# Three of eleven channel groups of gate and up as block products with seven multiplications of eight

## The chip, the cores and the metric

The kernel runs on one core of a Trainium2 chip. The core's engines are in-order queues that wait for one another through semaphores: TensorE (PE, matmuls, with weight loads listed apart as PEld), VectorE (DVE), ScalarE (ACT), GpSimd (POOL, used for a few operations and as a DMA queue) and SyncE (SP, a DMA queue). The metric is the device time of one execution in microseconds (us); less is better.

## The reference

One decoder layer over 256 tokens and 16 meta tokens in float32: an RWKV-7 branch and a forgetting-attention branch, a gated merge, the output projection w_o, and a SwiGLU feed-forward. The change lies in the last two:

```python
merged = g_a * (y_a @ w_a) + g_b * (y_b @ w_b)
h = h + merged @ w_o
gate, up = jnp.split(_rms(h, n2) @ w_gu, 2, axis=-1)
return h + (jax.nn.silu(gate) * up) @ w_dn
```

h has 2048 channels, gate and up have 5632 each, and w_gu is 2048 x 11264.

## The kernel before

Every matrix product is done to float32 accuracy in three matmuls: an operand is split into a rounded high part and the remainder (hi and lo), and hi x hi, lo x hi and hi x lo are added up in PSUM. Weights come in tiles of 128 x 1024 elements (512 KB): SP fetches one into raw (four buffers), ACT writes its high part wh, DVE subtracts to get wl (four buffers of each, so the preparation can be up to three tiles ahead of PE). The function run takes a list of jobs, each a load and a multiplication; it writes the load of the next job ahead of the multiplication of the one before. The order on each engine is that of a scheduler, which puts out instructions by its own estimate of when they are ready.

**w_o** (tm_jobs): tokens on the partitions, four groups of 512 channels, eight weight tiles each. The function post adds x into hh (the residual, two tiles of tokens, kept in SBUF to the end), sums its squares, turns it with PE transposes (hT), scales it by n2 (htmp), and splits it into hts, 16 channel tiles with a high and a low part of 256 tokens side by side. The norm's factor rs2 is spread over the partitions as rsb2 (spread, two transposes) and multiplied in after the product.

**Gate and up** (lines 1402 to 1423): eleven groups j of 512 columns, first gate (tile gt), then up (tile up), eight weight tiles each. PE holds a 128 x 128 piece of the weights and streams hts through it (mm2, lines 440 to 443): 512 columns against wh (both parts of hts in one matmul) and 256 against wl, so 16 + 16 matmuls in a tile. Gate accumulates in the four PSUM banks called main, up in the four called aux. At a group's end halves (lines 447, 448) adds the two halves of a bank (ACT copies, DVE adds); DVE multiplies by rsb2, ACT takes silu, and the product of gate and up is split into ach and acl (44 channel tiles, transposed: channels on the partitions).

**Down**: 22 blocks i of 256 channels. Twelve of them (SLOW) are plain. Ten (FAST) use a block product with seven multiplications for eight, which needs four sums of token quarters (sums_of_tokens, made at the end of an up group, written to DRAM as ss by POOL and fetched again as sst and into ach and acl) and sums of weight quarters (tt, from a fetch q). Before, FAST is 0 to 9, so the groups j = 0 to 4 make the sums. The results of the seven products are added to hh at the end of each half (sums_of_products).

Of the kernel before, what the change touches and what calls it, by code (L numbers as in the profile page):

```python
# [60 lines left out]
PLACE_T = (8, 16)  # L61

# [5 lines left out]
FAST = list(range(10))  # L68
SLOW = list(range(10, 22))
ORDER = [SLOW[:4] + [i for pair in zip(FAST, SLOW[4:] + FAST[-1:]) for i in pair],  # L70
         SLOW[:1] + [i for pair in zip(FAST, SLOW[1:]) for i in pair] + SLOW[11:]]
QUICK = [FAST[:-1], FAST]

# [42 lines left out]
def hybrid_block(ctx, tc, A, out, dbg=None):  # L116
# [1185 lines left out]
    hh = hp.tile([P, 2, D], F32, tag="hh", name="hh")  # L1302

    ht_pool = tc.tile_pool(name="ht", bufs=1, reuse_waits="tile")
    ht = ht_pool.__enter__()
    ht.tile([P, 32], F32, tag="shift", name="shift")
    hts = ht.tile([P, KT, 2, L], F32R, tag="hts", name="hts")
    ss2 = hp.tile([P, 2, 4], F32, tag="ss2", name="ss2")
    rs2 = hp.tile([P, 2], F32, tag="rs2", name="rs2")
    rsb2 = hp.tile([P, T], F32, tag="rsb2", name="rsb2")  # L1310

# [28 lines left out]
    for j in range(4):  # L1340
# [3 lines left out]
        def post(t, ps, j=j, js=js):  # L1344
            nc.vector.tensor_tensor(hh[:, t, js], ps, hh[:, t, js], op=ALU.add)
            jk = ht.tile([P, 512], F32, tag="jk", name=f"jk{j}{t}", bufs=2)
            nc.scalar.activation(jk, hh[:, t, js], AF.Square, accum_out=ss2[:, t, j:j + 1])
            if t == 0:
                return
            for k in range(4 * j, 4 * j + 4):  # L1350
# [3 lines left out]
                tmp = ht.tile([P, T], F32, tag="htmp", name=f"htmp{k}", bufs=3)  # L1354
                nc.vector.tensor_scalar(tmp, pt, vc("n2", k), None, op0=ALU.mult)
                split(hts[:, k, 0, NMETA:], hts[:, k, 1, NMETA:], tmp)
        run(tm_jobs(A["w_o"][0][:, js], KT, mgh, mgl, post, f"wo{j}"))
# [5 lines left out]
    obs = [ht.tile([P, P], F32, tag="ob", name=f"ob{t}", bufs=2) for t in range(2)]  # L1363
    for t in range(2):
        nc.vector.tensor_copy(obs[t], rs2[:, t:t + 1].to_broadcast([P, P]))

    def spread():

        prb = aux_ps("prb")[:, :T]
        for t in range(2):  # L1370
            pe_tr(prb[:, t * P:(t + 1) * P], obs[t], ident)
        nc.vector.tensor_copy(rsb2, prb)
        return
        yield
    spawn(spread(), SPREAD)
    dump("hh", hh)
# [11 lines left out]
    ssd = {}  # L1388

    def sums_of_tokens(i, u0, u1):  # L1390

        (a11, a21), (a12, a22) = ((u[:, :P], u[:, P:]) for u in (u0, u1))
        sx = ht.tile([P, 512], F32, tag="jk", name=f"sx{i}", bufs=2).rearrange("p (n c) -> p n c", n=4)
# [8 lines left out]
    for j in range(DFF // 512):  # L1402
        gs = [ht.tile([P, T], F32, tag="ga", name=f"ga{j}{m}", bufs=8) for m in range(4)]

        def post_gate(pss, gs=gs):
            for g, ps in zip(gs, pss):
                halves(g, ps)
                nc.vector.tensor_tensor(g, g, rsb2, op=ALU.mult)
                nc.scalar.activation(g, g, AF.Silu)
# [14 lines left out]

# [214 lines left out]
```

## Time and profile before

| | us |
|---|---|
| median of 3 runs | 1515.87 (1515.62 to 1516.62) |
| the profiled execution's own time | 1515.74 |
| its span, first to last instruction | 1514.0 |

| stage, us from the span's start | PE | DVE | ACT | share of DMA |
|---|---|---|---|---|
| 0 to 627, input projection and branches | 623.7 | 507.4 | 364.7 | 0.61 |
| 627 to 717, mostly branch projections | 90.0 | 62.4 | 43.2 | 0.73 |
| 854 to 1031, gate and up with token sums | 177.0 | 121.5 | 93.6 | 0.74 |
| 1031 to 1298, gate and up, start of down | 267.0 | 162.4 | 132.0 | 0.67 |
| 1298 to 1398, first half of down | 98.9 | 90.1 | 56.0 | 0.68 |
| 1398 to 1514, second half of down | 112.3 | 98.5 | 58.7 | 0.54 |

The table gives the busy time of each engine in each stage. "Busy" for PE counts a matmul until its modelled end, so it is the gaps that say something: a stage whose PE is busy for its whole length had no wait in front of a matmul. An answer of the trace has a start, a duration, the engine, the line, the operation with output <- inputs, and in brackets the idle time ahead of it with what ended that. A row of a window holds the bounds, the length, the busy times of PE, weight loads, DVE, ACT and POOL, the granted clock, the share of the DMA engines and GB/s.

### The profile page before, as it was taken

The page shows a single profiled execution, that of the slowest core. Times are in us where ns is not written, and L with a number is a line of the kernel's source. Part 1 is how long each engine was busy: PE and PEld are TensorE (multiplying, and loading weights), DVE is VectorE, ACT ScalarE, POOL GpSimd, SP SyncE. Part 2 cuts the span into 40 slices and gives each one's busy share as a digit, 9 for nine tenths or more (in the row PEclk, how much of TensorE's full clock was granted, in tenths as well). Part 3 has the DMA queues.
Part 4 walks back from the last instruction along what each step waited for, and adds up shares of the span by engine and source line. Part 5 has one row for each costly group of instructions (what it writes and reads, how often), then busy time and mean ns, then how long its engine had stood idle before and what let it go on. Part 6 is the DMA issues. An engine that isn't in the chain of part 4 may idle for free.

```text
span 1514.0 us, 26216 instructions
## 1 busy us (share of the span) xinstructions
PE 1505.9 (99%) x10056; PEld 1335.8 (88%) x10056; DVE 1130.9 (75%) x2014; ACT 817.8 (54%) x1234; POOL 123.5 (8%) x222
## 2 busy tenths in 40 slices
PE   9999999999999999999999999999999999999999
PEld 9999999999989888998888888888888888788887
DVE  7888699689779857875665776666566566789987
ACT  7664565475465545553555555555455455455553
POOL 2112202202202000000000000000000001000000
PEclk9999999999999999999999999999999999999999
DMA  8567456646645856777566777777666666966762
GB/s 272 166 167 212 119 155 183 173 118 178 189 126 149 224 153 204 241 257 216 181 182 183 227 219 226 208 214 214 195 186 189 195 185 207 326 197 202 224 213 86
DMA packets 214111, 293.82 MB, mean 194 GB/s; under 512 B 24737, under 2 KB 134833, under 8 KB 213985
## 3 DMA queue, kind: packets, MB, share of 16 engines
q1 hardware_dynamic: 202048, 277.25, 61.3%
q0 software_dynamic: 7040, 10.49, 2.2%
q10 hardware_dynamic: 4896, 4.40, 0.9%
q8 instruction: 79, 1.29, 0.3%
q14 instruction: 48, 0.39, 0.1%
HBM read 279.60 MB, written 12.49 MB: 193 GB/s over the span
## 4 chain that ended last, share of the span: by engine, by line
PE 97%; DVE 2%; DMA 0%; issue 0%; ACT 0%; SPq 0%; DVEq 0%
PE gt L441 11%; PE up L441 11%; PE zg L441 8%; PE gt L443 5%; PE up L443 5%; PE dn L1459 4%; PE dn L1457 4%; PE dn L1458 4%; PE zg L443 4%; PE f L441 2%; PE br L365 2%; PE br L366 2%; PE br L367 2%; PE f L365 2%; PE wo L1332 2%; PE wo L1334 2%
## 5 line engine op out<-in xcount | busy, mean ns | idle before, releaser
L336 DVE TENSOR_TENSOR wl<-raw,wh 128x1024 fp32r<-128x1024 f32 x450 | 550.2, 1227 | 271.7 <-ACT wh L335 270.6
L335 ACT ACTIVATE wh<-raw 128x1024 fp32r<-128x1024 f32 x450 | 475.7, 1059 | 442.4 <-PE up L441 121.8
L441 PE MATMUL gt<-hts,wh 128*128 128x512 f32 x704 | 243.0, 393 | 0.0
L441 PE MATMUL up<-hts,wh 128*128 128x512 f32 x704 | 242.7, 392 | 0.0
L443 PE MATMUL gt<-hts,wl 128*128 128x256 f32 x660 | 184.7, 280 | 0.0
L443 PE MATMUL up<-hts,wl 128*128 128x256 f32 x660 | 184.5, 280 | 0.0
L441 PE MATMUL zg<-xhl,wh 128*128 128x512 f32 x512 | 181.2, 399 | 0.0
L441 PEld LDWEIGHTS gt<-hts,wh 128*128 128x128 f32 x704 | 129.9, 188 | 25.2
L441 PEld LDWEIGHTS up<-hts,wh 128*128 128x128 f32 x704 | 129.9, 188 | 25.2
L443 PE MATMUL zg<-xhl,wl 128*128 128x256 f32 x480 | 134.3, 280 | 0.0
L443 PEld LDWEIGHTS up<-hts,wl 128*128 128x128 f32 x660 | 125.3, 190 | 1.8
L443 PEld LDWEIGHTS gt<-hts,wl 128*128 128x128 f32 x660 | 125.3, 190 | 1.8
L441 PEld LDWEIGHTS zg<-xhl,wh 128*128 128x128 f32 x512 | 94.3, 188 | 18.7 <-issue 0.7
L1457 PE MATMUL dn<-wh,ach 128*128 128x512 f32 x257 | 101.2, 394 | 0.0
L1459 PE MATMUL dn<-wl,ach 128*128 128x512 f32 x257 | 100.3, 393 | 0.6 <-DVE wl L511 0.4
L1458 PE MATMUL dn<-wh,acl 128*128 128x512 f32 x257 | 100.7, 392 | 0.0
L443 PEld LDWEIGHTS zg<-xhl,wl 128*128 128x128 f32 x480 | 90.9, 189 | 1.2
L365 PE MATMUL f<-xhl,wh 128*128 128x272 f32 x256 | 75.9, 296 | 0.0
L510 ACT ACTIVATE wh<-tt 128x1024 fp32r<-128x1024 f32 x38 | 40.4, 1063 | 64.9 <-PE dn L1458 60.0
L367 PE MATMUL f<-xhl,wl 128*128 128x272 f32 x256 | 73.6, 288 | 0.0
L366 PE MATMUL f<-xhl,wh 128*128 128x272 f32 x256 | 73.6, 288 | 0.0
L511 DVE TENSOR_TENSOR wl<-tt,wh 128x1024 fp32r<-128x1024 f32 x38 | 46.5, 1224 | 21.1 <-ACT wh L510 20.9
(496 smaller groups left out, 3171.0 us busy)
## 6 DMA issues: line engine op xcount, KB each, us to landing
raw<-in_w_gate_up_dram SPq DMA_DIRECT2D x176, 512.0 KB, 4.3
raw<-in_w_in_dram SPq DMA_DIRECT2D x160, 512.0 KB, 3.9
raw<-in_w_down_dram SPq DMA_DIRECT2D x50, 512.0 KB, 4.3
q<-in_w_down_dram SPq DMA_DIRECT2D x38, 512.0 KB, 5.0
raw<-in_w_o_dram SPq DMA_DIRECT2D x32, 512.0 KB, 4.4
raw<-in_w_branch_a_dram SPq DMA_DIRECT2D x16, 512.0 KB, 4.7
raw<-in_w_branch_b_dram SPq DMA_DIRECT2D x16, 512.0 KB, 4.7
ss<-sr POOLq DMA_DIRECT2D x10, 512.0 KB, 5.0
```

The source lines that it names most:

```text
L335: nc.scalar.activation(th, rr, AF.Copy)
L336: nc.vector.tensor_tensor(tl, rr, th.bitcast(F32), op=ALU.subtract)
L365: nc.tensor.matmul(ps, wh, ah, start=first, stop=False)
L366: nc.tensor.matmul(ps, wh, al, start=False, stop=False)
L367: nc.tensor.matmul(ps, wl, ah, start=False, stop=last)
L441: nc.tensor.matmul(ps.rearrange("p (a t) -> p a t", a=2), wh, act, start=first, stop=last)
L443: nc.tensor.matmul(ps[:, :T], wl, act[:, 0, :], start=False, stop=False)
L510: nc.scalar.activation(hi, src, AF.Copy)
L511: nc.vector.tensor_tensor(lo_, src, hi.bitcast(F32), op=ALU.subtract)
L1457: nc.tensor.matmul(o, a[0], hi, start=first, stop=False)
L1458: nc.tensor.matmul(o, a[1], hi, start=False, stop=False)
L1459: nc.tensor.matmul(o, a[0], lo_, start=False, stop=last)
```

## The change

Eight of the eleven groups (PLAIN, j = 0 to 7) stay as they were in their products. Three (BLOCK, j = 8 to 10) are computed with tokens on the partitions: a weight tile of 256 rows is taken as a block of two by two quarters (two of channels in, two of 256 columns), the tokens as two by two quarters (two of channels, two of 128 tokens), and seven products do for eight (groups bg for gate, bh for up). PE holds a 128 x 128 piece of tokens and streams 256 columns of weights; each of the seven products is three matmuls. Four aux banks hold the seven results of a group in halves, so a block group's gate and up follow one another on them. A weight tile is now prepared in two parts: 768 columns as fetched, and four quarters of sums (tt).

The sums of tokens that these products need are made in the w_o stage, at the end of each group (hs0 to hs7), written to DRAM by POOL and fetched to "homes": four tiles of their own and the parts of ach and acl where j = 6 and 7 will be stored. To make room, hh is written to DRAM (hhd, by ACT's queue) and fetched again in down (hh2). Gate and up of the plain groups both use main, and work on all 1024 elements of a group at once where they worked on 256 (except halves). At the end of a block group seven additions collect the products (sums); after up the result is turned by eight transposes (turn), and split into ach and acl. The block jobs are spread over the first 112 of the 128 plain jobs. FAST becomes 6 to 15, so that only plain groups (j = 3 to 7) make the sums for down.

```diff
-FAST = list(range(10))
-SLOW = list(range(10, 22))
+FAST = list(range(6, 16))
+SLOW = [i for i in range(22) if i not in FAST]
...
+PLAIN = list(range(8))
+BLOCK = list(range(8, 11))
+HOMES = 112
+FOLD = 9000
...
+    def sums_of_tokens(pool, tag, bufs, name, u0, u1, turned):
...
+        for n, x_, y_ in ((2, a11, a21), (3, a12, sx[:, 1])):
+            nc.vector.tensor_tensor(sx[:, n], x_, y_, op=ALU.subtract)
+        split(sr[:, 0], sr[:, 1], sx)
+        d = dp.tile([P, 2, 4, P], F32, tag=name, name=name)
+        nc.gpsimd.dma_start(d, sr.bitcast(F32))
+        return d
...
+            nc.scalar.dma_start(hhd[:, t, js], hh[:, t, js])
...
+                if k % 2:
+                    hsd.append(sums_of_tokens(wo, "hs", 2, f"hs{k // 2}", *tmps[-2:], True))
...
+    for h_, d in zip(homes, hsd):
+        nc.gpsimd.dma_start(h_, d)
...
+            nc.vector.tensor_tensor(g, g, rb, op=ALU.mult)
+            nc.scalar.activation(g, g, AF.Silu)
...
+            for i in range(2):
+                if 2 * j + i in FAST:
+                    ssd[2 * j + i] = sums_of_tokens(gu, "hb", 1, f"ss{2 * j + i}", ub[:, 2 * i], ub[:, 2 * i + 1],
+                                                    False)
...
+                def load0():
+                    raw = wp.tile([P, 1024], F32, tag="raw", name="raw", bufs=RAWB)
+                    nc.sync.dma_start(raw.rearrange("p (k c) -> p k c", c=512), kblock(src))
+                    w = parts(768)
+                    split(*w, raw[:, 256:])
+                    t = gu.tile([P, 1024], F32, tag="tt", name="tt", bufs=2)
...
+                def load1():
+                    w = parts(1024)
+                    split(*w, tt[0])
+                    return w
...
+                    nc.tensor.matmul(o, a[0], hi, start=opens, stop=False, skip_group_check=True)
+                    nc.tensor.matmul(o, a[1], hi, start=False, stop=False, skip_group_check=True)
+                    nc.tensor.matmul(o, a[0], lo_, start=False, stop=closes, skip_group_check=True)
...
+                def mul0(w):
...
+                    product("p1", token(i, 0, 0), w, 0)
+                    product("c12", s_of(3), w, 1)
+                    product("c11", token(i, 1, 0), w, 2)
+
+                def mul1(w):
+                    product("p5", s_of(0), w, 0)
+                    product("p7", s_of(2), w, 1)
+                    product("p6", s_of(1), w, 2)
+                    product("c21", token(i, 1, 1), w, 3)
...
+            for o, a, b in ((at(0, 0), ps["c11"], u), (u, ps["p6"], u), (v, ps["p5"], u), (at(0, 1), ps["c12"], v),
+                            (u, ps["p7"], u), (at(1, 0), ps["c21"], u), (at(1, 1), ps["p5"], u)):
+                nc.vector.tensor_tensor(o, a, b, op=ALU.add)
...
+        begin, stop = (HOMES * n // len(groups), HOMES * (n + 1) // len(groups))
+        for i, block in enumerate(g):
+            after = begin + 5 + (stop - begin - 6) * i // (len(g) - 1)
+            todo += plain[at:after]
+            at = after
+            todo += block
...
+        if cg == 0:
+            nc.gpsimd.dma_start(hh, hhd)
```

Three places show what moves. The first is PE in the fifth weight tile of the first gate group, from the two transposes of spread on; before, it reads:

```order
L395 MATMUL prb_10000<-ident_69,ob0_9868 128x128
L395 MATMUL prb_10000<-ident_69,ob1_9869 128x128
L441 MATMUL gt0_3_9899<-hts_9127,wh_9961 128x512
L443 MATMUL gt0_3_9899<-hts_9127,wl_9962 128x256
L441 MATMUL gt0_3_9899<-hts_9127,wh_9961 128x512
L443 MATMUL gt0_3_9899<-hts_9127,wl_9962 128x256
L441 MATMUL gt0_0_9896<-hts_9127,wh_9983 128x512
```

and now (bg82 and bg80 are the first block group's banks, home0 the first home):

```order
L400 MATMUL prb_10110<-ident_69,ob_9964 128x128 x2
L446 MATMUL gt0_3_10005<-hts_9129,wh_10067 128x512
L448 MATMUL gt0_3_10005<-hts_9129,wl_10068 128x256
L446 MATMUL gt0_3_10005<-hts_9129,wh_10067 128x512
L448 MATMUL gt0_3_10005<-hts_9129,wl_10068 128x256
L1500 MATMUL bg82_10124<-wh_10090,hts_9129 128x256
L1501 MATMUL bg82_10124<-wh_10090,hts_9129 128x256
L1502 MATMUL bg82_10124<-wl_10091,hts_9129 128x256
L1500 MATMUL bg80_10122<-wh_10090,home0_9967 128x256
```

The sixth plain tile has moved behind the first block tile, whose fourth matmul needs home0.

The second is the two engines that this block waits for. POOL's queue, from the sums of the last two w_o groups to the last home:

```order
L1430 DMA ach_9959<-hs4_9720 128x1024
L1430 DMA acl_9960<-hs5_9743 128x1024
L1334 DMA hs6_9914<-hs6r_9907 128x1024
L1334 DMA hs7_9937<-hs7r_9930 128x1024
L1430 DMA ach_9959<-hs6_9914 128x1024
L1430 DMA home0_9967<-hs0_9318 128x1024
L1430 DMA home1_9968<-hs1_9341 128x1024
```

and DVE at the same time (hs7r is the last sum of tokens, raw_10088 the first block's weights, tt its sums of quarters):

```order
L516 TENSOR_TENSOR hs7r_9930<-hs7r_9930 128x512
L1392 TENSOR_SCALAR ms2_9940<-rs2_9123 128x2
L516 TENSOR_TENSOR wl_10091<-raw_10088,wh_10090 128x768
...
L1482 TENSOR_TENSOR tt_10094<-raw_10088 128x512
L1482 TENSOR_TENSOR tt_10159<-raw_10153 128x512
L1486 TENSOR_TENSOR tt_10094<-raw_10088,tt_10094 128x256
L1418 COPY rsb2_9124<-prb_10110 128x256
L1487 TENSOR_TENSOR tt_10094<-raw_10088,tt_10094 128x256
L1486 TENSOR_TENSOR tt_10159<-raw_10153,tt_10159 128x256
L1487 TENSOR_TENSOR tt_10159<-raw_10153,tt_10159 128x256
L516 TENSOR_TENSOR wl_10119<-tt_10094,wh_10118 128x1024
```

None of these rows but the norm's stood here before. home0, though its data is written long before, stands behind a fetch of hs6, which waits for the write of hs6; and the first tt row waits for the writes of hs6 and hs7, whose memory it takes.

The third is SP's queue at the start of down, around the first fetch for a fast block (q). Before:

```order
L326 DMA raw_14698<-in_w_down_dram 128x2x512
L326 DMA raw_14710<-in_w_down_dram 128x2x512
L1488 DMA q00_14477<-in_w_down_dram 128x1024 x2
L1488 DMA q01_14643<-in_w_down_dram 128x1024 x2
L326 DMA raw_14779<-in_w_down_dram 128x2x512
```

and now:

```order
L331 DMA raw_15198<-in_w_down_dram 128x2x512
L331 DMA raw_15210<-in_w_down_dram 128x2x512
L331 DMA raw_15279<-in_w_down_dram 128x2x512
L331 DMA raw_15291<-in_w_down_dram 128x2x512
L1637 DMA q06_14976<-in_w_down_dram 128x1024 x2
L1637 DMA q07_15143<-in_w_down_dram 128x1024 x2
```

The q fetches have moved behind two more weight fetches, each of which waits until DVE has given back a raw buffer.

More of the change, by code (lines that the diff above doesn't have):

```diff
@@ L61 @@
 PLACE_T = (8, 16)
+SHIFT = 128
 LANES = 108
@@ L1301, in hybrid_block @@
     hp = hp_pool.__enter__()
[L1302 to L1307, printed above, removed]
     ss2 = hp.tile([P, 2, 4], F32, tag="ss2", name="ss2")
@@ L1362, in hybrid_block @@
     rsqrt_small(hp, rs2, ms2, [P, 2], "rst2")
[L1363 to L1376, printed above, removed]
+    wo_pool.__exit__(None, None, None)
     mg_pool.__exit__(None, None, None)
@@ L1402, in hybrid_block @@
[L1402 to L1409, printed above, removed]
-        def post_up(pss, gs=gs, j=j):
-            us = []
-            for m, (g, ps) in enumerate(zip(gs, pss)):
-                ub = ht.tile([P, T], F32, tag="ub", name=f"ub{j}{m}", bufs=2)
-                halves(ub, ps)
-                nc.vector.tensor_tensor(ub, ub, rsb2, op=ALU.mult)
-                nc.vector.tensor_tensor(ub, ub, g, op=ALU.mult)
-                split(ach[:, 4 * j + m, :], acl[:, 4 * j + m, :], ub)
-                us.append(ub)
-                if m % 2 and 2 * j + m // 2 in FAST:
-                    sums_of_tokens(2 * j + m // 2, *us[m - 1:])
-        run(cm_jobs(wgu[:, j * 512:(j + 1) * 512], KT, hts, NMETA, T, post_gate, name=f"gt{j}"))
-        run(cm_jobs(wgu[:, DFF + j * 512:DFF + (j + 1) * 512], KT, hts, NMETA, T, post_up, alloc=aux_ps, name=f"up{j}"))
+    gu_pool = tc.tile_pool(name="gu", bufs=1, reuse_waits="tile")
@@ new lines, in hybrid_block, with spread, home @@
+    gu = gu_pool.__enter__()
+    obs = gu.tile([P, 2, P], F32, tag="bu", name="ob")
+    for t in range(2):
+        nc.vector.tensor_copy(obs[:, t], rs2[:, t:t + 1].to_broadcast([P, P]))
+    def spread():
+        prb = aux_ps("prb")[:, :T]
+        for t in range(2):
+            pe_tr(prb[:, t * P:(t + 1) * P], obs[:, t], ident)
+        nc.vector.tensor_copy(rsb2, prb)
+        return
+        yield
+    spawn(spread(), SPREAD)
+    def home(t):
+        return t.rearrange("p (a n c) -> p a n c", a=2, n=4)
@@ L1431, in hybrid_block @@
+    plain = [job for j in PLAIN for job in plain_jobs(j)]
+    groups = [g for j in BLOCK for g in block_jobs(j)]
+    todo, at = [], 0
+    for n, g in enumerate(groups):
+        begin, stop = (HOMES * n // len(groups), HOMES * (n + 1) // len(groups))
[4 more added lines that the diff above has]
+            todo += block
+    run(todo + plain[at:])
     wdn = A["w_down"][0]
@@ L1438, in hybrid_block @@
     sst = dn.tile([P, len(fast), 2, 3, P], F32R, tag="sst", name="sst")
+    hh = dn.tile([P, 2, D], F32, tag="hh", name="hh2")
     def sums_of(i):
```

119 lines of the change are left out of this document (107 added, 12 removed).

## The prediction

> **What bounds the kernel now.** I read the page's busy line and chain first, then the windows of the stages, then the rows of the stage that is changed.
>
> ```profile
> span 1514.0 us, 26216 instructions
> PE 1505.9 (99%) x10056; PEld 1335.8 (88%) x10056; DVE 1130.9 (75%) x2014; ACT 817.8 (54%) x1234; POOL 123.5 (8%) x222
> PE 97%; DVE 2%; DMA 0%; issue 0%; ACT 0%; SPq 0%; DVEq 0%
> 831.87:1275.87 444.00, 444.00 (x2561) 391.57 (x2561) 288.62 (x450) 228.75 (x331) 15.25 (x28) 1.00 0.69 204
> 831.87 0.46 PE up L441 x2
> 1275.87 0.46 PE up L441 x2
> ```
>
> TensorE (PE) is 97% of the chain of waits that ended last. In the window over most of gate and up it has no idle time, at the full clock, and VectorE (DVE, third pair of numbers) works 288.6 of 444 us, 65%. The last two rows, of the chain, are the same place in the first and in the last up group, twenty groups of eight weight tiles apart: 444.0 / 160 = **2.775 us of PE for one plain weight tile**. A change here is worth what it takes off PE, less every wait that it puts in front of PE.
>
> **What PE gains.** Of 11 x 16 tiles, 48 become block tiles. Each plain one is 16 matmuls of 512 columns and 16 of 256. Each block tile is 21 matmuls of 256 columns, each with its own weight load. The branch stage already runs such a stream:
>
> ```profile
> 605.87:697.31 91.44, 91.44 (x774) 91.35 (x773) 70.03 (x89) 47.63 (x50) 0.00 (x0) 1.00 0.76 249
> 650.01 0.28 PE L365 MATMUL br<-ybs,wh 128*128 128x256 f32 x1
> 651.43 0.28 PE L365 MATMUL br<-ybs,wh 128*128 128x256 f32 x1
> 788.48 0.39 PE L441 MATMUL gt<-hts,wh 128*128 128x512 f32 x1
> 790.07 0.40 PE L441 MATMUL gt<-hts,wh 128*128 128x512 f32 x1
> ```
>
> Between the two br rows lie 12 matmuls: 1.42 / 12 = 0.1183 us each. A block tile takes 21 x 0.1183 = 2.484 us, and saves 0.291. The window says why it isn't the eighth that counting columns promises (0.347): weight loads are busy 91.35 of 91.44 us. So 48 x 0.291 = **-14.0 us**. Unequal column patterns could move the pitch; bounds are the 0.347 of the count (-16.7) and a gain of half (-7).
>
> The page "TensorE: Matmul & The Clock Gate" of the Trainium skill, section "Back-to-back issue gap", gives N/2.4 + 2.5 ns for a lone matmul, 109 ns at 256 columns; by it a block tile takes 2.29 us and the change saves 23 us. The same section says that in a stream of load and matmul both set the spacing, and the 118 ns of the br rows agree with that, so the row is used.
>
> PE is also given 24 transposes (turn, eight for each of three channel groups). From 788.48 to 790.07 stand two pairs of plain matmuls (2 x 0.347) and eight transposes: (1.59 - 0.69) / 8 = 0.112, so **+2.7 us**. Bare PE time falls by 11.3.
>
> **What DVE gets.** A plain tile costs DVE one subtraction of 1024 elements; a block tile costs 768, 512, 256, 256 and 1024.
>
> ```profile
> 1305.26 2.35 DVE L336 TENSOR_TENSOR wl<-raw,wh 128x1024 fp32r<-128x1024 f32 x2
> 1307.53 0.68 DVE L511 TENSOR_TENSOR wl<-q,wh 128x512 fp32r<-128x512 f32 x1
> 1308.13 0.68 DVE L1512 TENSOR_TENSOR tt<-q,tt 128x512 f32<-128x512 f32 x1
> 811.36 0.74 DVE L448 TENSOR_TENSOR ga<-ga,gt 128x256 f32<-128x256 f32 x2
> 812.03 0.75 DVE L1408 TENSOR_TENSOR ga<-ga,rsb 128x256 f32<-128x256 f32 x2
> L1396 DVE TENSOR_TENSOR sx<-ub,ub 128x128 f32<-128x128 f32 x10 | 2.8, 285 | 0.0
> 1335.00:1355.00 20.00, 20.00 (x88) 16.30 (x87) 17.22 (x19) 10.95 (x12) 0.00 (x0) 1.00 0.63 209
> 1300.00:1310.00 10.00, 9.07 (x39) 6.78 (x38) 9.93 (x11) 6.00 (x7) 0.00 (x0) 1.00 1.04 351
> ```
>
> From start to start back to back: 1024 elements 2.27 / 2 = 1.135, 512 0.60, 256 0.67 / 2 = 0.335, and 0.87 between for 768; 128 as listed, 0.285. A block tile: 0.87 + 0.60 + 0.67 + 1.135 = 3.28. The stage after: 128 plain tiles 145.3; 48 block tiles 157.4; eight plain posts of eight 256 and four 1024 57.6; three block posts of fourteen 256 and four 512 21.3; ten token sums of four 128 and one 512 17.4. That is 399 us beside PE's 128 x 2.775 + 48 x 2.484 + 2.7 = 477, or **84%**. With the listed durations instead of start to start, as for rows that wait for the row ahead, it is some 443, 93%. The down stage is the measure: at 17.22 of 20, 86%, PE loses nothing; at 9.93 of 10 it loses 0.93. So DVE's sum as such is charged nothing, and what stops DVE in its order is.
>
> One such stop is new: the two sums of a plain block now share one buffer (hb), so the second one's first subtraction waits until the first one's write has landed, and all weight tiles queue behind it on DVE. The write and the next instruction that needs it:
>
> ```profile
> 841.16 0.78 POOL L1400 DMA_DIRECT2D ss<-sr  x1 [307.62 <-DVE sr L511]
> 845.94 0.55 POOL L1443 DMA_DIRECT2D ach<-ss  x1 [4.00 <-DMA ss<-sr]
> ```
>
> 4.8 us, against some three weight rows between (3 x 1.135 = 3.4): up to 1.4 us of DVE lost, five times. DVE is up to three tiles (about 8 us) ahead of PE, and spends that on the burst of the up post just there. I charge half, **+3.5 us**, between 0 (the lead covers it) and 19 (the third rival).
>
> **The first block.** In before the last split of hts ends at 794.95, and the first group begins at 788.48. POOL writes hs6 and hs7 from there and fetches the homes behind them.
>
> ```profile
> 790.68 1.26 DVE L1355 TENSOR_SCALAR htmp<-hT,vcol 128x256 f32<-128x256 f32 x3
> 794.53 0.42 DVE L511 TENSOR_TENSOR hts<-htmp,hts 128x256 fp32r<-128x256 f32 x1
> sst<-ss POOLq DMA_DIRECT2D x10, 384.0 KB, 13.3
> ```
>
> PE reaches the block after five tiles, eight transposes and two of spread: 788.5 + 5 x 2.775 + 1.2 = 803.6, and asks for home0 0.35 us later. DVE ahead of the hs6 write: from 790.7 on eight htmp and hts rows of about 0.36, seven subtractions of 0.285 and a split of 0.60, so 796. The write lands at 800.9, the queue then issues ach (which waits for it) and home0 at about 801.5, and home0 lands 4.8 later, at 806.3: PE waits 2.4. With the 13.3 us that ten loads together took, it is 814.8 and 10.9. Five loads of 512 KB go out in a row here, nearer to one than to ten: **+4 us**. At the same time DVE stands at tt, whose memory waits for the hs6 and hs7 writes (until 803), and then has 4.4 us of rows to the block's second tile: 807.4, hidden behind home0.
>
> **The rest.** Gate and up now both accumulate in main, so ten plain groups follow one another on the same banks.
>
> ```profile
> 810.09 0.37 ACT L447 ACTIVATE ga<-gt 128x256 f32<-128x256 f32 x1
> 811.99 0.23 PE up L441
> ```
>
> In before the first bank was read out by 811.36 + 0.41 = 811.77, and the next group began at 811.99: covered by 0.2, with the four additions now together. If DVE is one weight row late it costs 0.9 each, ten times; I take 0.5 in all with the 3.5 above. In the w_o stage eight sums add some 15 us of DVE over 92 us:
>
> ```profile
> 717.00:809.00 92.00, 92.00 (x445) 75.98 (x444) 58.27 (x86) 44.37 (x64) 0.00 (x0) 1.00 0.61 183
> ```
>
> 58.3 + 15 is 80%, below the 86% that cost nothing: 0. Its cover is the three tiles ahead (8 us) over a burst of 6.
>
> At the start of down the first fast block already waits in before:
>
> ```profile
> 1286.71 2.20 SPq L1488 DMA_DIRECT2D q<-in_w_down_dram  x4
> 1296.34 0.63 ACT L510 ACTIVATE wh<-q 128x512 fp32r<-128x512 f32 x1 [6.17 <-DMA q<-in_w_down_dram]
> 1300.12 0.47 issue
> 1303.28 0.84 issue
> q<-in_w_down_dram SPq DMA_DIRECT2D x38, 512.0 KB, 5.0
> ```
>
> The q fetch now stands behind two more weight fetches on SP, which wait for DVE: some 4.7 us later. But sst waits for ss15, written late, so q no longer lands in its burst (9.6 us here, 5.0 in the last row, the median of all). **+1 us**, between -1.3 (both waits gone) and +4.7. The 2 MB of hh2 ride behind sst and are wanted some 90 us later: 0.
>
> **Sum** against the profiled execution's own time, 1515.74 (span 1514.0 and 1.7 around it; median of the runs 1515.87): 1515.7 - 14.0 + 2.7 + 3.5 + 4 + 0.5 + 1 = **1513.4, say 1513**. That is -0.2%, just where a measurement of this kernel begins to tell a change from none (some 0.2%, 3 us).
>
> **Rivals.** *The waits are covered*: home0 at its 2.4 or less, the DVE stops inside the lead, down's wait as before: 1515.7 - 11.3 + 2.4 = 1507, or 1504 where column counting holds. For it: 84% of DVE; against: seven new places at which DVE or PE must wait for a landing. *The change doesn't do what it says*: loads out of homes or the contiguous tiles slow the stream; at 2.775 / 21 = 0.132 us a matmul the gain is gone, and the time is 1515.7 + 2.7 + 9 = 1527. No row of 256 or 272 columns in the trace is that slow. *DVE becomes the bound*: between the start of one block group and its end stand 12 or 13 plain and 8 block tiles, PE 53 to 56 us; DVE 12 x 1.135 + 8 x 3.28 = 40, plus an up post with sums of 8.2, a gate post of 2.5 and stops of 1.4: 52. At j = 3 and later that is 95% and over. From there the 1300:1310 row sets the price, 0.93 us in 10: over half of the stage's 430 us with blocks, 20 us in place of the 3.5, so 1513 + 16 = 1529; with a quarter, 1520.
>
> ```profile
> 1500.00:1514.00 14.00, 10.27 (x45) 8.06 (x43) 8.78 (x14) 0.09 (x1) 0.00 (x0) 0.97 0.21 75
> ```
>
> A further mechanism rides on the first block: where PE stands idle some 3.7 us, in this last window, the granted clock's mean is 0.97; it is 1.00 in all windows above. A wait of 4 us there could cost 1 to 2 us more, 1515. The skill's page named above, section "What's actually happening", has PE at half clock after an idle window of about 3.4 us; this trace has no idle stretch inside the work to test that.
>
> **How the numbers follow.** My forecast (1509 to 1518, with the clock step) 0.48; waits covered (1503 to 1509) 0.25; DVE the bound (1518 to 1530) 0.20; no gain in PE 0.07. The range leaves out the top and a little of the bottom: 1504 to 1521. Faster by over 0.2% (below 1512.8): 0.25 and nearly half of the forecast's 0.48, 0.45. Within 0.2%: 0.29. Slower (above 1518.9): 0.26.
>
> **What would show it.** A pitch of 0.118 between bg and bh matmuls; PE idle once for 2 to 6 us at the first block, released by the DMA of home0; DVE over 85% from there to the last block, with stops at the second sum until a landing; the q wait at the start of down. It is wrong if PE idles at every group's start (banks), or if DVE's share nears 100% with PE waiting for wl throughout.

## The result, and the profile after

| | before | after |
|---|---|---|
| median of 4 runs each, us | 1515.75 (1515.62 to 1516.62) | 1531.91 (1529.78 to 1533.32) |
| ratio, with 95% interval | | 1.0104 (1.0087 to 1.0122) |
| span of the profiled execution, us | 1514.0 | 1531.6 |
| PE time that the matmuls of gate and up need without a wait, us | 490.1 | 478.3 |
| length of gate and up, us | 489.6 | 499.6 |
| length of down, us | 231.8 | 237.8 |

The change makes the kernel 1.0% slower. The forecast was 1513, between 1504 and 1521, and had the sign wrong. First the busy line of the page after:

```profile
PE 1507.4 (98%) x10320; PEld 1345.4 (88%) x10320; DVE 1234.6 (81%) x2132; ACT 844.9 (55%) x1212; POOL 133.5 (9%) x239
```

PE still seems to be busy for 98%, since a matmul at half clock, or one that waits inside its modelled length, counts as busy. So the whole stretch is read from start to start: the distance of each PE row to the next, less the pitch of its form (0.230 us for 512 columns, 0.117 for 256, 0.118 for 256 in a block tile, 0.112 for a transpose). What is left over is called the **excess** below. In one block tile of the timeline of PE there is none:

```profile
886.65 0.39 PE L446 MATMUL gt<-hts,wh 128*128 128x512 f32 x1
...
889.25 0.28 PE L1502 MATMUL bh<-wl,hts 128*128 128x256 f32 x1
889.37 0.39 PE L446 MATMUL up<-hts,wh 128*128 128x512 f32 x1
```

From the last gt row to the first up row lie 2.72 us, one matmul of 512 (0.23) and 21 block matmuls: 2.49, as forecast. The loss stands at three places. The waits of PE, from its timeline:

```profile
809.28 0.55 PE L1500 MATMUL bg<-wh,home 128*128 128x256 f32 x1 [3.65 <-DMA home<-hs]
1137.31 0.39 PE L1502 MATMUL bg<-wl,ach 128*128 128x256 f32 x1 [1.40 <-DVE wl L516]
1176.15 0.50 PE L446 MATMUL gt<-hts,wh 128*128 128x512 f32 x1 [1.43 <-DVE ub L453]
1210.81 0.50 PE L446 MATMUL up<-hts,wh 128*128 128x512 f32 x1 [1.44 <-DVE ga L453]
1318.30 0.76 PE L1606 MATMUL dnp<-wh,sst 128*128 128x512 f32 x1 [3.04 <-DMA sst<-ss]
```

The first is the wait for home0 at the first block; the next three are the longest of some fifteen from 915 us on, behind weight tiles (wl) and the readout of banks (ga, ub); the last is the late sst at the start of down. Windows of before and after (length, PE, weight loads, DVE, ACT, POOL, clock, DMA share, GB/s), first of before over the place of the first block, then of after over the same place, behind the wait for home0, over the rest of gate and up, and behind the wait for sst:

```profile
790.00:815.00 25.00, 25.00 (x147) 22.05 (x147) 18.04 (x39) 13.67 (x23) 0.00 (x0) 1.00 0.63 184
```

```profile
790.00:815.00 25.00, 21.35 (x119) 19.01 (x118) 20.00 (x48) 11.62 (x18) 5.38 (x10) 0.86 0.99 327
812.00:815.00 3.00, 3.00 (x13) 2.71 (x13) 2.63 (x3) 1.09 (x2) 0.00 (x0) 0.50 1.05 375
915.00:1280.00 365.00, 356.40 (x2265) 320.01 (x2264) 303.89 (x427) 201.73 (x247) 12.85 (x24) 1.00 0.66 203
1318.00:1322.00 4.00, 3.70 (x9) 2.95 (x10) 3.93 (x4) 3.31 (x4) 2.78 (x5) 0.50 1.30 403
```

The DMA engines are full at the first block (0.63 before, 0.99 after), the clock is at one half behind both long waits, and from 915 to 1280 us VectorE is busy for 303.9 of 365 us, 83%. In excess: 6.7 us in the first 50 of gate and up, 14.4 from 126 us on to its end, 8.0 in down (before: 0, -0.5 and 2.0). With PE's 11.8 less that is 16 us more, and the profiled execution is 17.6 longer; the rest is a start of gate and up 1.6 later, which the runs below, with the same program up to there, don't all show (787.9 to 789.5 us).

What stands behind the waits is seen on ScalarE and VectorE. Their waits of more than 10 us in all, 915 to 1280 us and 815 to 1290 us (total, times, longest):

```profile
ACT wh L515 <- DVE tt L1487: 45.4, 21, 4.7
ACT wh L340 <- PE up L446: 35.1, 21, 3.1
ACT wh L340 <- PE gt L446: 17.9, 10, 4.3
```

```profile
DVE tt L1482 <- DMA raw<-in_w_gate_up_dram: 37.2, 24, 3.8
DVE wl L341 <- ACT wh L340: 20.5, 21, 1.6
DVE wl L516 <- ACT wh L515: 20.2, 26, 1.3
```

A wait for PE is harmless: the buffers are full. The other two are new. ScalarE stands at the wh of a block's second part until VectorE has written tt, with the wh of later tiles queued behind it; and VectorE stands at the first tt row until its fetch has landed, with wl rows and readouts behind it. The three longest waits of PE from 915 us on, at 1137, 1176 and 1211 us, each follow such a stop of VectorE:

```profile
1135.42 0.69 DVE L1482 TENSOR_TENSOR tt<-raw 128x512 f32<-128x512 f32 x1 [3.80 <-DMA raw<-in_w_gate_up_dram]
1174.21 0.69 DVE L1482 TENSOR_TENSOR tt<-raw 128x512 f32<-128x512 f32 x1 [1.78 <-DMA raw<-in_w_gate_up_dram]
1204.66 0.69 DVE L1482 TENSOR_TENSOR tt<-raw 128x512 f32<-128x512 f32 x1 [2.90 <-DMA raw<-in_w_gate_up_dram]
```

Behind each of them VectorE works without a wait up to the row that PE waits for. The experiments ask which of these costs the time: VectorE's load (B), its order (E1), or the chain fetch, tt, wh, wl through both engines (E2).

### The profile page after: what moved, and what is told of

It reads as the page before. It is cut to its first block, busy times and chain, and to the rows that moved or that the text cites. A ratio compares the mean times of both kernels' runs of the same rounds, so it can differ in the third digit from the quotient of the medians.

```text
span 1531.6 us, 26983 instructions
## 1 busy us (share of the span) xinstructions
PE 1507.4 (98%) x10320; PEld 1345.4 (88%) x10320; DVE 1234.6 (81%) x2132; ACT 844.9 (55%) x1212; POOL 133.5 (9%) x239
## 5 line engine op out<-in xcount | busy, mean ns | idle before, releaser
L340 ACT ACTIVATE wh<-raw 128x1024 fp32r<-128x1024 f32 x402 | 423.1, 1057 | 318.8 <-PE up L446 52.2
L341 DVE TENSOR_TENSOR wl<-raw,wh 128x1024 fp32r<-128x1024 f32 x402 | 489.6, 1226 | 115.8 <-ACT wh L340 114.6
L446 PE MATMUL gt<-hts,wh 128*128 128x512 f32 x512 | 179.3, 396 | 1.7 <-DVE ub L453 1.7
L446 PE MATMUL up<-hts,wh 128*128 128x512 f32 x512 | 178.4, 394 | 2.1 <-DVE ga L453 2.1
L515 ACT ACTIVATE wh<-tt 128x1024 fp32r<-128x1024 f32 x86 | 91.4, 1063 | 143.4 <-DVE tt L1487 64.4
L516 DVE TENSOR_TENSOR wl<-tt,wh 128x1024 fp32r<-128x1024 f32 x86 | 105.2, 1223 | 38.8 <-ACT wh L515 37.1
L448 PE MATMUL gt<-hts,wl 128*128 128x256 f32 x480 | 134.1, 282 | 0.6 <-DVE wl L341 0.6
L448 PE MATMUL up<-hts,wl 128*128 128x256 f32 x480 | 133.9, 280 | 0.3 <-DVE wl L341 0.3
L446 PEld LDWEIGHTS up<-hts,wh 128*128 128x128 f32 x512 | 94.3, 188 | 20.5 <-DVE ga L453 3.2
L446 PEld LDWEIGHTS gt<-hts,wh 128*128 128x128 f32 x512 | 94.5, 189 | 19.7 <-DVE ub L453 2.7
```

Source lines behind the costliest of these rows:

```text
L340: nc.scalar.activation(th, rr, AF.Copy)
L341: nc.vector.tensor_tensor(tl, rr, th.bitcast(F32), op=ALU.subtract)
L446: nc.tensor.matmul(ps.rearrange("p (a t) -> p a t", a=2), wh, act, start=first, stop=last)
L448: nc.tensor.matmul(ps[:, :T], wl, act[:, 0, :], start=False, stop=False)
L515: nc.scalar.activation(hi, src, AF.Copy)
L516: nc.vector.tensor_tensor(lo_, src, hi.bitcast(F32), op=ALU.subtract)
```

## Experiments

All edits are to the changed kernel. Excess is that of the profiled execution, in us: first 50 us of gate and up, from 126 us on, and down; "ACT at tt" is ScalarE's wait at the second part's wh from 915 to 1290 us. Kernels with blocks scatter by 1 to 8 us between executions (before mostly by about 1), and an excess is that of one execution, so a difference of a few us in one of them says little by itself.

| run | median, us | ratio to before | first 50 | from 126 | down | ACT at tt |
|---|---|---|---|---|---|---|
| after | 1531.9 | 1.0104 (1.0087 to 1.0122) | 6.7 | 14.4 | 8.0 | 45.4 |
| e1 sums early | 1530.1 | 1.0094 (1.0080 to 1.0108) | 6.9 | 16.8 | 2.8 | 42.7 |
| e2 first block later | 1535.5 | 1.0127 (1.0113 to 1.0141) | 7.3 | 16.3 | 7.2 | 58.2 |
| e3 tt in turn | 1542.6 | 1.0176 (1.0162 to 1.0190) | 6.1 | 22.6 | 10.8 | 94.0 |
| e4 and own raw | 1548.8 | 1.0218 (1.0204 to 1.0232) | 15.9 | 20.9 | 7.4 | 97.6 |
| e5 no quarter sums | 1523.6 | 1.0048 (1.0033 to 1.0063) | 6.4 | 2.3 | 10.9 | none |
| e6 sums of ready data | 1522.4 | 1.0042 (1.0027 to 1.0057) | 6.1 | 6.9 | 6.8 | none |
| e7 tt on POOL | 1544.9 | 1.0183 (1.0166 to 1.0200) | 8.6 | 26.4 | 8.4 | 47.1 |
| e8 no token sums | 1519.7 | 1.0021 (1.0010 to 1.0032) | 5.2 | 13.1 | 0.7 | 40.0 |
| e9 six raw | 1537.4 | 1.0144 (1.0129 to 1.0160) | 8.9 | 11.7 | 8.3 | 10.8 |
| e10 tt memory, later | 1536.2 | 1.0130 (1.0116 to 1.0144) | 7.9 | 18.7 | 8.1 | 56.7 |
| e11 e9, e10, sums earlier | 1532.5 | 1.0112 (1.0098 to 1.0127) | 9.6 | 19.3 | 4.5 | 20.8 |
| e12 plain tile between | 1525.8 | 1.0062 (1.0048 to 1.0076) | 6.3 | 7.9 | 7.5 | 11.1 |
| e13 e12 and e3 | 1541.6 | 1.0158 (1.0144 to 1.0173) | 5.3 | 19.3 | 10.5 | 78.3 |
| e14 e13, eight raw | 1539.9 | 1.0154 (1.0141 to 1.0168) | 9.0 | 16.7 | 8.0 | 87.5 |
| e15 e14, e10, sums earlier | 1542.1 | 1.0169 (1.0155 to 1.0183) | 8.9 | 25.9 | 2.8 | 69.5 |
| e16 e12, block at 12 | 1531.6 | 1.0104 (1.0090 to 1.0118) | 11.2 | 9.7 | 7.9 | 11.7 |
| e17 e16, room for sums | 1527.7 | 1.0077 (1.0064 to 1.0089) | 10.0 | 10.4 | 5.5 | 28.1 |
| e18 e17, sums early | 1527.1 | 1.0082 (1.0069 to 1.0096) | 9.3 | 9.2 | 4.3 | 32.3 |

**One place each (e1 to e4).** e1:

```diff
-FAST = list(range(6, 16))
+FAST = list(range(10))
```

> FAST is 0 to 9 again, as before the change, so the sums for down are made in the plain groups j = 0 to 4 and are long written when down begins; everything else as in the changed kernel (median 1531.9 us). Theory A (what the change loses is several separate waits, and one of them is the late sst: 3.04 us at the first sst row, 0.8 behind it, and 2 more at half clock): the excess over the pitch at the start of down falls from 8.0 to about 2, the gate and up stage keeps its excess of 21 us, total about 1526 to 1527. Rival B (VectorE is simply overloaded in gate and up): the excess there moves from j = 4 to 7 to j = 0 to 4 and stays of the same size; the start of down still gains, so B gives the same total; but with A the waits stay where block tiles are, with B they go where the sums are. Rival C (down starts late because of its weight fetch q, queued behind gate and up's last fetches): no change in down, 1531 to 1532.

Down's excess fell from 8.0 to 2.8, as A said, but gate and up lost 2.7 more, where the sums now stand. The transfers of POOL show why sst is late in the changed kernel, and not in e1:

```profile
1309.20 0.54 POOL L1334 DMA_DIRECT2D ss<-ss15r  x1 [1.14 <-DVE ss15r L516]
1309.73 3.52 POOL L1590 DMA_DIRECT2D sst<-ss  x5
```

```profile
1292.07 4.92 POOL L1590 DMA_DIRECT2D sst<-ss  x7 [157.50 <-PE up L446]
```

In the changed kernel sst queues on POOL behind the last sum's write, 20 us after down began (1289.7); in e1 it goes out half a microsecond after (1291.6). The late sst is shown, and worth 5 us there. The median keeps 2 of it, which can't be told from none, since the intervals overlap.

e2:

```diff
-        begin, stop = (HOMES * n // len(groups), HOMES * (n + 1) // len(groups))
+        begin, stop = 4 + 18 * n, 22 + 18 * n
```

> The first block tile comes after 9 plain tiles in place of 5 (groups begin at 4 + 18 n of the plain jobs; the last block keeps its place), so home0 is wanted some 11 us later than the 809.3 at which it landed. Theory A: the wait of 3.65 us at home0 goes, and with it the stretch at half clock behind it (about 3 us): 1531.9 - 6.7 = about 1525. If the lower clock there has another cause than the wait: -3.7 only, 1528. If the homes only come later too, or the wait moves to another operand of the block (tt, wl): no change, 1531 to 1532.

The wait for home0 went, and PE waited 4.88 us, up to 816.6, for the readout of the first gate group instead. The forecast missed; e10 and e16 take it up.

e3 makes the sums in raw itself, whose quarters are r0 to r3 (the places of p6 and p7 are exchanged to suit); e4 is the same with two raw buffers of the blocks' own, braw:

```diff
-                    t = gu.tile([P, 1024], F32, tag="tt", name="tt", bufs=2)
...
+                    for o, a, b, op in ((r2, r2, r0, ALU.subtract), (r0, r1, r0, ALU.subtract), (r1, r1, r2, ALU.add),
+                                        (r3, r3, r1, ALU.subtract)):
+                        nc.vector.tensor_tensor(o, a, b, op=op)
```

> The sums of weight quarters are made in place in raw, in such an order that the first of them overwrites what the tile's own wl row reads: so VectorE can't stand at a block's tt row ahead of the wl rows of the tiles before it. Four rows of 256 in place of 512, 256, 256 (+0.07 us a block, 3.5 us of VectorE in all); raw is held a little longer, still four buffers. Theory A (head-of-line: VectorE stood 65 us in the changed kernel at the first tt row until its fetch landed, with wl and readout rows behind it that were ready): those stops fall under 15 us and PE's excess from 915 us to the end of gate and up from 14.6 to under 5: about 1521 to 1523. Rival B (VectorE's sum, 84 to 87% busy): its work is the same or 3 us more, so PE waits as much, 1531 to 1535. Rival D (four raw buffers are too few for block tiles): the stops stay, but at the wl rows, PE's excess 10 or more, 1528 to 1533.

> As the run with the sums of weight quarters in place and in turn, and block tiles have two raw buffers of their own (the memory that tt left free), so six in all. Theory A: like that run, or up to 2 us less: 1520 to 1523. Rival B (VectorE's sum): 1531 to 1535 as there. Rival D (four raw buffers are too few): only this run gains, PE's excess from 915 us on under 5, 1521, while the run with four buffers stays at 1528 or more.

VectorE no longer stands at tt for a landing, just as meant, and both are slower, by 11 and 17 us. What grew is the waits of ScalarE and VectorE for each other (e3, ScalarE from 915 to 1280 us, VectorE from 815 to 1290):

```profile
ACT wh L515 <- DVE raw L1484: 94.0, 31, 5.0
ACT ach L515 <- DVE ub L1447: 11.1, 3, 4.3
```

```profile
DVE wl L516 <- ACT wh L515: 55.6, 45, 2.9
```

The first sum overwrites a quarter of raw that the first part's wl still reads, and that wl row waits for its wh. So the way is now fetch, wh, wl, sums, wh, wl: the sums come later, and ScalarE waits for them twice as long as in the changed kernel. Its wh of the second part starts 2.5 us ahead of the matmul that uses it, against 4.7 there (means of the last 40 block tiles, from the timelines). In e4 the blocks' raw also lies over the memory of the last token sums, so the first block waits 9.7 us.

**Load or chain (e5 to e8).** e5 leaves the three tt rows out (the sums of weight quarters) and splits raw itself for the second part; e6 does so too and keeps three rows of the same size, computed from the wl just written (y), that nobody reads:

```diff
-                    nc.vector.tensor_tensor(t[:, :512].rearrange("p (x c) -> p x c", x=2),
...
+                    y = w[1].bitcast(F32)
+                    nc.vector.tensor_tensor(t[:, :512], y[:, :512], y[:, 256:], op=ALU.subtract)
+                    nc.vector.tensor_tensor(t[:, 512:768], y[:, 512:], t[:, :256], op=ALU.add)
+                    nc.vector.tensor_tensor(t[:, 768:], y[:, 512:], t[:, 512:768], op=ALU.subtract)
```

> Leaves out the sums of weight quarters (the three tt rows of each of 48 block tiles); the second part of a block tile is split from raw itself, so PE, the weight splits, the posts and all transfers stay. VectorE loses 48 x 1.27 = 61 us of work from start to start, and the two-step chain fetch, tt, wh, wl becomes fetch, wh, wl. Theory B (VectorE's work in the stage) and theory E (the chain: ScalarE's wh of the second part waits for tt on VectorE, and wl for that wh, each in order with other rows) both say that PE's excess from 915 us to the end of gate and up falls from 14.6 to under 3: 1531.9 - 12 = about 1520; the wait for home0 and the late sst stay. If the waits come from elsewhere (banks, fetches), 1528 to 1532.

> The same three VectorE rows in each block tile, of the same sizes, but computed from the tile's own wl, which VectorE has just written, and read by nobody; the second part is split from raw. So VectorE's work is that of the changed kernel, while nothing waits for a fetch in these rows and no chain runs through them. Theory B (work): PE waits as in the changed kernel, excess from 915 us on 10 to 16, 1528 to 1533. Theory E (the chain and VectorE's order): like the run without the rows, about 1520, excess under 5.

The windows of e5 and e6:

```profile
915.00:1275.00 360.00, 359.07 (x2306) 325.90 (x2305) 264.76 (x326) 207.21 (x252) 12.85 (x24) 1.00 0.69 209
```

```profile
915.00:1280.00 365.00, 362.19 (x2310) 326.49 (x2309) 308.74 (x432) 207.40 (x255) 12.84 (x24) 1.00 0.68 206
```

VectorE is busy for 74% in e5 and for 85% in e6, a little more than in the changed kernel (83%). The excess is 2.3 and 6.9, against 14.4. So the way of tt through the engines is worth 7 to 8 us, and both medians lie 8 to 10 us below the changed kernel's. The load alone is worth 4 to 5 by these two executions, but the medians (1523.6 and 1522.4) don't show it, since e5 loses 4 us more at the start of down. Either way B is not the main cause.

e7 does the three rows on POOL:

```diff
-                    nc.vector.tensor_tensor(t[:, 512:768], raw[:, 512:768], t[:, :256], op=ALU.add)
+                    nc.gpsimd.tensor_tensor(t[:, 512:768], raw[:, 512:768], t[:, :256], op=ALU.add)
...
```

> The three tt rows go to POOL, which has nothing else to compute in this stage (3 us of transfers in 80). VectorE loses 61 us of work, 84 to about 72%; the chain stays and gets longer: POOL's rows of 256 and 272 elements take 0.73 to 0.98 us in the branch stage, so some 2.9 us for a block in place of 1.27. Theory B (work): excess from 915 us on under 4, 1519 to 1522. Theory E (chain): as in the changed kernel or worse, 1530 to 1540.

A loss of 13 us. ScalarE waits 47.1 us for tt as before, and VectorE's plain wl rows became longer, in the groups of e7 and of the changed kernel:

```profile
L341 DVE TENSOR_TENSOR wl<-raw,wh 128x1024 fp32r<-128x1024 f32 x120 | 170.0, 1427 | 42.7 <-ACT wh L340 42.0
```

```profile
L341 DVE TENSOR_TENSOR wl<-raw,wh 128x1024 fp32r<-128x1024 f32 x125 | 151.3, 1219 | 20.7 <-ACT wh L340 20.5
```

e8 leaves out the token sums for down; POOL writes the product ub in their place:

```diff
-                    ssd[2 * j + i] = sums_of_tokens(gu, "hb", 1, f"ss{2 * j + i}", ub[:, 2 * i], ub[:, 2 * i + 1],
...
+                    nc.gpsimd.dma_start(ssd[2 * j + i], home(ub.rearrange("p m c -> p (m c)")))
```

> Leaves out the ten token sums of the plain groups (four rows of 128 and one of 512 on VectorE, one of 512 on ScalarE each): POOL writes the product itself in their place, so all transfers stay. VectorE loses 17 us of work, in j = 3 to 7 alone. Theory B (work, at its densest there): the waits of the later half fall by a half or more, excess from 1090 us to the end of the stage from 10 to 5 or less, and sst comes about 2 us earlier: 1523 to 1526. Theory E (chain): excess there stays at 8 to 10, total 1529 to 1532.

12 us faster (ten runs, from 1516.0 to 1523.8), but mostly not where B put it: 7.3 of it are the start of down, where sst is no longer late; gate and up lost 18.6 in place of 21.3.

**Raw buffers and memory (e9 to e11).** e9: homes 0 and 1 alone stay in tiles of their own, two more go where j = 10 is stored, and load0's raw comes from two buffers of the blocks' own.

```diff
-    homes = [home(gu.tile([P, 1024], F32R, tag=f"home{i}", name=f"home{i}")) for i in range(4)]
-    for j in PLAIN[-2:]:
+    homes = [home(gu.tile([P, 1024], F32R, tag=f"home{i}", name=f"home{i}")) for i in range(2)]
+    for j in PLAIN[-2:] + BLOCK[-1:]:
...
-                    raw = wp.tile([P, 1024], F32, tag="raw", name="raw", bufs=RAWB)
+                    raw = gu.tile([P, 1024], F32, tag="braw", name="braw", bufs=2)
```

> Block tiles have two raw buffers of their own (six in all); the sums of weight quarters stay as in the changed kernel (three rows, into tt). The memory comes from two homes that move into the part of ach and acl where j = 10 will be stored. Theory E (VectorE stands in its order at tt until a fetch lands that was issued late, since four raw buffers were taken): fetches go out some two tiles earlier, VectorE's stops at tt fall from 65 to under 15 us, PE's excess from 915 us to the end of the stage from 14.6 to 5 or 6 (what is left with the same work and no chain): about 1523. Rival F (the time is lost in the chain tt, wh, wl itself, whatever the fetch does): excess stays at 10 or more, 1528 to 1532.

e10 is e2 with tt allocated first in its pool; e11 joins e9 and e10 (with braw first beside tt) and has FAST 4 to 13:

```diff
+    gu.tile([P, 1024], F32, tag="tt", name="tt", bufs=2)
     obs = gu.tile([P, 2, P], F32, tag="bu", name="ob")
```

> The first block comes 4 plain tiles later (as in e2), and tt lies first in its pool, over hh, no longer over the buffers from which the last token sums hs6 and hs7 are written. Theory G (the first block is held twice, PE by home0's landing and VectorE by tt's memory, which waits for the hs7 write to land; taking one away leaves the other): excess of the first 50 us falls from 6.7 to under 1, total about 1525 to 1526. If the tt memory was not what held VectorE in e2: 5 us or more of excess stay there, 1531 to 1535.

> Both of the above (six raw buffers, tt and the raw of the blocks first in the pool, first block later) and the sums for down in j = 2 to 6 (FAST 4 to 13) in place of 3 to 7, so that the last plain group makes none. Theories E and G with the late sst: 1531.9 - 9 (chain) - 6 (first block) - 5 (start of down) = 1512, below the kernel before the change. Rival F (chain stays): 1520 to 1523. Rival B' (denser sums beside the blocks of j = 8 and 9 give back 3, as with FAST 0 to 9): 1515.

All three missed. With six buffers VectorE still waits 24.5 us at tt from 915 us on (27.6 in the changed kernel): the scheduler moved tt up its order with the fetch, so that the first tt row starts 17.6 us ahead of its matmul on average, against 9.4. ScalarE's wait for tt fell to 10.8 us, and what PE now waits for is the readout of banks, which stands behind those tt rows on VectorE:

```profile
1080.75 0.50 PE L446 MATMUL up<-hts,wh 128*128 128x512 f32 x1 [1.53 <-DVE ga L453]
1207.19 0.50 PE L446 MATMUL up<-hts,wh 128*128 128x512 f32 x1 [1.46 <-DVE ga L453]
```

Of PE's waits from 915 us to the end of gate and up, readouts are 5.4 of 7.1 us in e9 and 9.0 of 12.4 in e11, against 3.8 of 8.6 in the changed kernel. Tt's memory was not what held VectorE in e2, since e10 reads just the same.

**A tile between the two parts (e12 to e15).** e12:

```diff
-            todo += block
+            todo += [block[0], *plain[at:at + 1], block[1]]
+            at += 1
```

> The two parts of each block tile are multiplied with one plain tile between them, so ScalarE's wh and VectorE's wl of the second part come a plain tile (2.8 us of PE) after the first; the tt rows themselves still stand where the scheduler puts them, ahead of other rows. Theory E1 (VectorE's order: tt ahead of ready rows, until its fetch lands): stops at tt stay (30 us or more after 815 us), PE's excess from 915 us on 10 to 15, 1527 to 1533. Theory E2 (latency of the chain tt, wh, wl): excess falls under 6, 1520 to 1523.

6 us faster than the changed kernel, with intervals apart. The waits of ScalarE and VectorE in e12 (915 to 1280, and 815 to 1290 us):

```profile
ACT wh L515 <- DVE tt L1487: 11.1, 7, 3.7
```

```profile
DVE tt L1482 <- DMA raw<-in_w_gate_up_dram: 28.3, 25, 2.4
```

ScalarE's wait for tt fell to a quarter, while VectorE stopped at tt as often as before (25 times against 24), if shorter (28.3 us against 37.2). The excess from 126 us on is 7.9, of which 4.1 lie at one place near the end (1254 us), so it comes down to that of e6. That is between the two forecasts, under 6 (E2) and 10 to 15 (E1), and nearer to E2. But it doesn't rule E1 out: the distance also gives VectorE's stops more room (the first tt row starts 12.2 us ahead of its matmul), and PE's waits for readouts fell with the others, from 3.8 to 0.5 us. What e6 and e12 show is that the time goes where the second part follows at once on the first, through its fetch, tt on VectorE, wh on ScalarE and wl on VectorE, each in its engine's order. How it divides between VectorE's stop and ScalarE's wait they don't show.

> A plain tile between the two parts, and the sums in place behind the tile's own wl row (as in e3, four raw buffers). If both order and chain hold (each of the two repairs leaves the other's loss): the excess from 915 us on falls under 6 here, though e3 alone had 19: 1521 to 1524. If the second part's raw, held a plain tile longer, holds up the fetches: stops at wl for a landing, 10 or more of excess, 1530 to 1538.

> As the run with a plain tile between and the sums in turn, with four raw buffers for block tiles beside the four of plain tiles (memory from tt and from two homes moved into ach and acl at j = 10). If held raw buffers delay the fetches there, only this run gets the excess from 915 us on under 6. The blocks' first buffers may lie over the last token sums' memory, so the first block can start later: 1520 to 1530 in all.

> As e14, with the blocks' raw first in its pool, the first block 4 plain tiles later, and the sums for down in j = 2 to 6. With order and chain both repaired, VectorE no longer stands at a tt row ahead of the first bank readout (the 4.9 us of e2 and e10 at 812 us): excess of the first 50 us under 2, from 915 us on under 6, down's 4.5 as in e11: 1531.9 - 5 - 9 - 3.5 = about 1514. If the density of VectorE's work decides after all (75 to 80 us of 90 in e11), 1522 or more.

e13 is e12 with e3's sums; e14 has four raw buffers of the blocks' own (in the room of tt and of two homes, as in e9); e15 adds FAST 4 to 13, the later first block of e2, and the blocks' raw first in the pool. All three missed and came out 8 to 10 us above the changed kernel: with the sums behind wl ScalarE waits 70 to 88 us for them even with a tile between. It isn't for lack of raw buffers: e14 has twice as many.

**The first block (e16 to e18).** e16 is e12 with groups that start at 7 + 17.5 n; e17 gives the token sums two buffers of their own (a tag sb in place of hb, in the room of two homes as in e9) and sets FOLD to 12000; e18 has FAST 0 to 9 as well.

```diff
-        begin, stop = (HOMES * n // len(groups), HOMES * (n + 1) // len(groups))
+        begin, stop = 7 + 105 * n // 6, 7 + 105 * (n + 1) // 6
...
-                    ssd[2 * j + i] = sums_of_tokens(gu, "hb", 1, f"ss{2 * j + i}", ub[:, 2 * i], ub[:, 2 * i + 1],
+                    ssd[2 * j + i] = sums_of_tokens(gu, "sb", 2, f"ss{2 * j + i}", ub[:, 2 * i], ub[:, 2 * i + 1],
```

> The plain tile between the two parts (as e12), and the first block after 12 plain tiles in place of 5 (groups 17.5 plain tiles long, the last block where it was): the first gate group's banks are read out before the second block's tt, and the homes' burst is over. Theory G2 (in e2 and e10 the first block's loss only moved to the readout behind a tt row that waited for a fetch slowed by the burst): excess of the first 50 us falls from 6.3 to under 2, 1525.8 - 5 = about 1521. If it only moves again: 1525 to 1528.

> As e16, and the token sums have two buffers of their own (from two homes that move into ach and acl at j = 10) in place of the one shared with hb, and the turn of a block group comes 3 us later. VectorE's stops at the second sum (3.5 us at ss13r in e12, 4.2 in e13), the wait of 2.1 us at bt, and some of the late sst (ss15 is written 3 us earlier) should go: 2 to 5 us below e16, 1516 to 1519. If these stops were covered: as e16.

> As e17, with the sums for down in j = 0 to 4 (FAST 0 to 9): down's excess as in e1 (2.8, against 7.5 in e12), and up to 3 us given back where the sums now stand beside the blocks of j = 8 and 9: 1513 to 1517, the first that could reach the kernel before the change. If the density of VectorE's work at j = 1 to 4 costs more than the start of down: 1518 to 1522.

The first block's loss can't be moved away like this: it grew from 6.3 to 11.2 us. The timelines of SP, VectorE and PE in e16:

```profile
805.37 0.37 SPq L1477 DMA_DIRECT2D raw<-in_w_gate_up_dram  x1
```

```profile
816.91 0.69 DVE L1482 TENSOR_TENSOR tt<-raw 128x512 f32<-128x512 f32 x1 [8.77 <-DMA raw<-in_w_gate_up_dram]
819.12 1.40 DVE L453 TENSOR_TENSOR ga<-ga,gt 128x256 f32<-128x256 f32 x4
```

```profile
819.58 0.80 PE L446 MATMUL up<-hts,wh 128*128 128x512 f32 x1 [8.18 <-DVE ga L453]
790.00:815.00 25.00, 21.40 (x124) 18.57 (x122) 15.06 (x39) 13.16 (x21) 4.30 (x8) 1.00 1.06 378
```

A weight fetch issued at 805.37 had landed when VectorE went on at 816.91, 11.5 us later, amid the homes' 4 MB, with the DMA engines full (1.06); VectorE stood at tt for it, and the readout of the first gate group queued behind. The median landing of these fetches is 4.5 us in the changed kernel. So home0 seems to be one face of it, and whatever PE wants first waits for the burst. That the burst slowed this fetch is read from these rows; no run takes the burst away. Own buffers for the sums took the stops at the second sum away and gained nothing in gate and up (10.4 against 9.7); the start of down gained 2.4 and e17 is 4 us faster than e16. Of the complete versions e12 is the fastest, 1525.8; none reaches the kernel before.

## Why the prediction was wrong, step by step

- **PE's gain**: right. -11.8 us measured (490.1 to 478.3) against -11.3 forecast, at the pitch of the br rows. A plain tile is 8 matmuls of 512 columns and 8 of 256, not 16 and 16 as written ahead of the result (2.775 / 0.347 = 8); the sum went by the measured 2.775 and is untouched by that.
- **First block, +4**: right in place and releaser, mis-sized: 6.7. The wait was 3.8; 2.9 more went at half clock behind it. The forecast named that step at 1 to 2 us, and counted it in the upper bound of its case only.
- **VectorE's sum charged nothing, its order 3.5, banks 0.5**: this step failed. In place of 4 us stand 14.9 (from -0.5 to 14.4). VectorE's share came out as forecast, 83% against 84%, and the sum as such is worth 4 to 5 at most (e6 against e5); taking away the shared hb, to which the 3.5 were charged, gained nothing there (e17). What was left out is the way of tt: the forecast never followed the second part of a block tile from its fetch through tt on VectorE and wh on ScalarE back to wl. It priced tt as so many microseconds of VectorE, and neither as a row at which VectorE stands for a fetch (37.2 us) nor as a link between two queues (45.4 us of ScalarE). The 0.5 for banks belongs to the same step: readouts are 3.8 us of PE's waits. Taking this way out is worth 7 to 8 (e6), and e12, which changes no row's length, takes back 6.5.
- **Start of down, +1**: mis-sized: 6.0 (2.0 to 8.0). That ss15 is written late was seen, but weighed against q's burst; in POOL's order the sst fetches come behind that write, and half the clock goes with the wait (e1, e8).
- **w_o and the 2 MB of hh2, 0**: no wait is seen at either.
- **Rivals**: "VectorE becomes the bound", 1520 to 1529, came nearest in time, and for another reason: at 85% in e6 PE lost 6.9 us, not 20.

Read together, the runs show a trade between the two links. e3 and e13 take away VectorE's stop at tt and pay with ScalarE's wait (94 and 78 us). e9 and e11 put tt early, take away most of ScalarE's wait, and pay with late readouts (excess 11.7 and 19.3). e12 eases both, and e6 takes both out. Three things stay open: how the changed kernel's loss divides between the two, since the runs that take one away make the other worse; the first block, where the burst is the likely cause and no run removes it; and why e9's profiled execution (1530.9) was so much faster than its median (1537.4).

## What to carry to other kernels

A sum that is computed on one engine and split by another ties two in-order queues together: follow such a tile through every queue it passes, and ask at each what is queued behind it, rather than adding up busy time by engine. Where two parts of a tile depend on each other, multiply something else between them. A burst of transfers is priced by the bytes that all queues move in it, weight fetches included, not by the transfer one is waiting for.

## What the hardware showed unexpectedly

**The clock.** A wait of some 2 us can halve it. In e12, from the windows:

```profile
1253.00:1256.00 3.00, 0.87 (x6) 0.58 (x5) 2.86 (x7) 0.39 (x2) 1.07 (x2) 0.98 0.96 302
1256.00:1259.00 3.00, 3.00 (x11) 2.42 (x12) 2.48 (x7) 1.33 (x2) 0.00 (x0) 0.50 0.18 43
```

PE stood for 2.1 us, and ran the next 3 us at 0.50. Over all profiles, of 44 waits of PE between 0.9 and 1.65 us that stood alone one was followed by half clock (1.53 us, in e15); of those between 1.7 and 2.8 us about half were (14 of 25); of the 26 longer ones all. The clock records say why a wait of 2 us does it only at times. In each run all stretches of half clock start on one grid of 3.41 us, and 48 of the 52 last one or two of its steps. What counts is how long PE stood within one step: above 1.9 us half clock followed every time, below 1.4 once. A stretch costs some 1.5 to 3 us, as an estimate from half of the time in it in which PE works. The Trainium skill, "TensorE: Matmul & The Clock Gate", section "What's actually happening", gives an idle window of about 3.4 us that runs freely. The grid agrees with that; but in these runs the window need not be idle throughout, 1.9 of its 3.41 us are enough.

**POOL beside VectorE.** With tt on POOL, VectorE's subtraction of 1024 elements took 1427 ns on average in place of 1219 (e7), and a tt row of 512 took 1778 ns on POOL against 688 on VectorE. The Trainium skill, "SBUF — State Buffer", section "Who interferes with whom", says that a VectorE instruction with two inputs in SBUF contends with a GpSimd instruction that reads SBUF; VectorE's longer rows agree.
